# A two-layer encoder trunk on one core: the second overflow test of a block of four experts moves ahead of gather, sums and transposes

## Chip, core and metric

The kernel runs on one core of one Trainium2 chip. The metric is the device time of one execution in microseconds (us), as the median of three runs. The core has five engines: TensorE (PE, its weight loads shown as PEld), VectorE (DVE), ScalarE (ACT), GpSimd (POOL) and SyncE (SP), which here issues the weight transfers. Each has a queue of its own, and an engine works through its queue in order.

## What is computed

Input x is 256 tokens of 1024 float32 values. Two layers follow each other, each with a token mixer and a mixture of 32 experts, and a last normalisation. The change lies in the experts (`hier_moe` of the reference, cut):

```python
g_idx = argmax(xt @ w_rg + b_rg)                 # one of 4 groups per token
top_v, top_i = lax.top_k(e_sel, 2)               # two of the group's 8 experts
gate = ...                                       # 256 x 32, two values per token, the rest 0
for g in range(4):
    h = silu(xt @ w_gate[g]) * (xt @ w_up[g])    # 1024 -> 256, per expert
    h = h * gate[:, g]
    y = y + h @ w_down[g]                        # 256 -> 1024, per expert
x = x + y
```

So each token needs two experts of 32. How many tokens an expert gets is known only once the router has run on the chip.

## The kernel before

**Blocks and slots.** Instead of all 256 tokens, each expert gets a fixed number of token slots. The experts of a layer are worked off in nine blocks, in an order written out by hand (`ORDER`): seven blocks of four experts with 32 slots each, and two blocks of two experts with 64 each. In layer 1 the order is (16, 17), (0 to 3), (18, 19), (4 to 7), (8 to 11), (12 to 15), (20 to 23), (24 to 27), (28 to 31); the text counts these blocks from 0 to 8. The slots of a block fill the 128 rows of TensorE, in four column groups of 32 or two of 64.

**Steps of a block**, in program order:
- `fill_slots` (line 1335 on): transposes of the weighted one-hot table, then ScalarE (line 1341) and VectorE (1342) make the slots' gate values `gs` and the 0/1 matrix `Sm` that maps slots to tokens.
- `gate_up` (line 1442): the gate and up projections into the PSUM tile `gu`, in two halves of the 1024 inputs, one weight page per expert and half. A float32 matmul leaves two records in the trace, so a half has 32.
- `hidden` (1345 on): Silu on ScalarE (1347), then the product with `gs` on VectorE (1348), into the scratch page `scr`.
- Where the next block belongs to a new group: `gather` (1236), which picks that block's tokens with one-hot matrices on TensorE; ScalarE and VectorE evict by turns (`either`, 355 and 359).
- `combine` (1245 on) of the block **before**: its results, kept as a high and a low part, both of the type fp32r, in a `y` page, are summed back to tokens by single-pass matmuls with `Sm` (1251 for the high, 1252 for the low part), and VectorE adds them to x (1253). It comes in two parts, and between them stands `hidden_t`: two transposes of the hidden values (line 372) and their copy by ScalarE (1356).
- `down` (1458): the down projection, in two halves of 512 columns of 32 records each, every half followed by `split_y`: ScalarE writes the high part (1360), VectorE the low part (1361).

**Overflow.** An expert of a block of four may have more than 32 tokens. Slots 33 to 64 are worked off by `second`, under a test of a flag that the router computed (`more`). It stands in two places: the first test (line 1559) between the two halves of `gate_up`, in which the guarded work builds one-hot tables, gathers (1474), fills slots and runs the first half of gate/up for the overflow tokens; the second test (line 1589) ahead of `down`, in which it runs the second half, `hidden`, `hidden_t`, `down` and `combine`. The guarded work has a PSUM tile of its own (`gu2`), but shares `scr` and the `y` page with its block. A test is one unit on all five engines: each branches, and where the flag is 0 PE, DVE and ACT execute one semaphore instruction on the skip path. An expert with more than 64 tokens gets a further stage, the units (tests at line 1424, unit work from 1381 on), once per layer, behind block 3 of layer 0 and block 5 of layer 1.

**Order.** The framework puts the instructions of each engine in an order of its own, close to program order; ready work is put ahead of a test that isn't ready. A test itself is not split, and nothing of its body moves out of it.

**Weights.** All weights stream from HBM through SP into a ring of 25 pages of 1 MB (`pump`, line 227 on). `done` (258) gives a page back behind its last reader and starts the next transfers; a page that a guarded part reads comes free behind the test. `work_page` takes pages of the same ring for `scr`, `y` and the like.

The second test, as it stands before:

```python
y = w["y"] = y_page()
...
if quad:
    with tc.If(more > 0):
        for hf in range(0 if b == 0 else 1, 2):
            second(blk, w, hf)
    done(*[(l, "gu", e, hf) for hf in range(0 if b == 0 else 1, 2) for e in blk])
fn = final(Sm, *y) if end and b == len(blks) - 1 else None
pend = (Sm,) + down(blk, hT, y, next(fn) if fn else None)
```

## Time and profile before

| what | value |
|---|---|
| device time, median of 3 runs | 740.88 us (740.05 to 741.61) |
| profiled execution | 737.13 us |
| its span on the core | 735.4 us |
| PE busy | 631.6 us (86%) |
| DVE busy | 373.7 us (51%) |
| ACT busy | 253.2 us (34%) |
| POOL busy | 107.5 us (15%) |
| moved by DMA | 232.90 MB, mean 317 GB/s |

The profile is of one execution. Its slices cut the span in 40 equal parts of 18.4 us. A line such as L1458 is the program line whose instructions it counts. Behind a duration, `[2.86 <-DVEq L1589]` says that the engine stood idle for 2.86 us before, and that what ended last by the trace was VectorE's queue at line 1589. A name with q (PEq, DVEq, SPq) is an engine's sequencer: branches, semaphores and the issue of transfers.

### The profile page before, as it was taken

The page shows a single profiled execution, that of the slowest core. Times are in us where ns is not written, and L with a number is a line of the kernel's source. Part 1 is how long each engine was busy: PE and PEld are TensorE (multiplying, and loading weights), DVE is VectorE, ACT ScalarE, POOL GpSimd, SP SyncE. Part 2 cuts the span into 40 slices and gives each one's busy share as a digit, 9 for nine tenths or more (in the row PEclk, how much of TensorE's full clock was granted, in tenths as well). Part 3 has the DMA queues.
Part 4 walks back from the last instruction along what each step waited for, and adds up shares of the span by engine and source line. Part 5 has one row for each costly group of instructions (what it writes and reads, how often), then busy time and mean ns, then how long its engine had stood idle before and what let it go on. Part 6 is the DMA issues. An engine that isn't in the chain of part 4 may idle for free. (4 is left out here: it accounts for less than half of the span.)

```text
span 735.4 us, 12004 instructions
## 1 busy us (share of the span) xinstructions
PE 631.6 (86%) x4370; PEld 386.3 (53%) x4370; DVE 373.7 (51%) x899; ACT 253.2 (34%) x578; POOL 107.5 (15%) x135
## 2 busy tenths in 40 slices
PE   7997989889799498598799899989899987769994
PEld 6584877744245334336268677775444434324442
DVE  3899977532334117824279878752423324322424
ACT  3647873421012014524074397352111211001113
POOL 1202001000000021521051754510000000000001
PEclk9999999999899799889999999989999999979998
DMA  8920375896999899999994715895999999998992
GB/s 304 419 108 0 117 289 215 331 389 231 413 406 416 280 405 411 412 415 407 398 417 183 286 59 172 302 362 194 333 416 406 392 410 413 416 366 301 410 382 83
DMA packets 57207, 232.90 MB, mean 317 GB/s; under 512 B 6048, under 2 KB 8480, under 8 KB 48160
## 3 DMA queue, kind: packets, MB, share of 16 engines
q1 hardware_dynamic: 57120, 231.75, 81.5%
q8 instruction: 53, 0.87, 0.5%
q14 instruction: 34, 0.28, 0.1%
HBM read 233.82 MB, written 1.05 MB: 319 GB/s over the span
## 5 line engine op out<-in xcount | busy, mean ns | idle before, releaser
L1442 PE MATMUL gu<-pg,xe 128*32 128x512 f32 (+1 forms) x1024 | 147.9, 618 | 12.4 <-DMA pg<-in_w_up_dram 7.1
L1458 PE MATMUL yp<-pg,scr 128*32 128x512 f32 (+2 forms) x560 | 79.4, 639 | 25.9 <-DVEq L1589 11.5
L1442 PEld LDWEIGHTS gu<-pg,xe 128*32 128x32 f32 (+1 forms) x1024 | 48.1, 117 | 96.7 <-issue 91.0
L1236 PE MATMUL gp<-oh,xn 128*128 128x128 f32 (+1 forms) x416 | 71.2, 325 | 4.0 <-DVE oh L1221 2.0
L1236 PEld LDWEIGHTS gp<-oh,xn 128*128 128x128 f32 x416 | 61.4, 197 | 18.6 <-issue 10.6
L1458 PEld LDWEIGHTS yp<-pg,scr 128*32 128x32 f32 (+1 forms) x560 | 22.1, 120 | 73.0 <-issue 58.2
L1361 DVE TENSOR_TENSOR y<-yp,y 128x512 fp32r<-128x512 f32 (+1 forms) x39 | 26.3, 677 | 65.8 <-ACT y L1360 65.8
L1348 DVE SCALAR_TENSOR_TENSOR scr<-gu,gs,scr 128x256 f32<-128x256 f32 x19 | 9.1, 481 | 97.1 <-ACT scr L1347 97.1
L1228 POOL TENSOR_TENSOR pgt<-oh,gate 128x256 f32<-128x256 f32 (+1 forms) x13 | 10.2, 783 | 316.5 <-PE slp L372 304.6
L1253 DVE TENSOR_TENSOR x<-cp,x 128x512 f32<-128x512 f32 x76 | 48.9, 685 | 14.2 <-PE cp L1252 14.2
L1360 ACT CAST y<-yp 128x512 fp32r<-128x512 f32 (+1 forms) x39 | 22.3, 575 | 88.1 <-PE yp L1458 86.6
L359 DVE TENSOR_SCALAR xe<-gp,vec 128x128 f32<-128x128 f32 (+1 forms) x52 | 20.8, 400 | 52.0 <-PE gp L1236 52.0
L355 ACT ACTIVATE xe<-gp,vec 128x128 f32<-128x128 f32 (+1 forms) x52 | 21.3, 409 | 73.3 <-PE gp L1236 73.2
L1347 ACT ACTIVATE scr<-gu 128x256 f32<-128x256 f32 x19 | 7.3, 384 | 102.3 <-PEq L1559 52.3
L1251 PE MATMUL cp<-y,sm 128*128 128x512 f32 x76 | 34.0, 455 | 0.3 <-PEq L1559 0.2
L1252 PE MATMUL cp<-y,sm 128*128 128x512 f32 x76 | 30.4, 409 | 1.5 <-DVE y L1361 1.5
L1058 DVE SCALAR_TENSOR_TENSOR x<-op,rg,x 128x512 f32<-128x512 f32 x24 | 17.9, 749 | 16.8 <-PE op L681 11.9
L1341 ACT ACTIVATE scr<-slp 128x256 f32<-128x256 f32 x20 | 7.8, 388 | 42.2 <-SPq L1424 28.8
L1251 PEld LDWEIGHTS cp<-y,sm 128*128 128x128 f32 x76 | 14.5, 192 | 10.4 <-issue 8.2
L372 PE MATMUL hp<-cst,scr 128*128 128x128 f32 x40 | 9.3, 314 | 12.2 <-DVE scr L1348 11.1
L372 PE MATMUL slp<-cst,pgt 128*128 128x128 f32 x36 | 8.3, 314 | 11.2 <-DVEq L1424 5.9
L1252 PEld LDWEIGHTS cp<-y,sm 128*128 128x128 f32 x76 | 14.3, 193 | 5.5 <-DVE y L1361 3.8
(454 smaller groups left out, 1209.2 us busy)
## 6 DMA issues: line engine op xcount, KB each, us to landing
pg<-in_w_gate_dram SPq DMA_DIRECT2D x128, 512.0 KB, 10.1
pg<-in_w_up_dram SPq DMA_DIRECT2D x128, 512.0 KB, 10.4
pg<-in_w_down_dram SPq DMA_DIRECT2D x56, 1024.0 KB, 11.8
pg<-in_w_o_dram SPq DMA_DIRECT2D x8, 1024.0 KB, 18.0
pg<-in_w_down_dram SPq DMA_DIRECT2D x12, 512.0 KB, 10.4
pg<-in_w_qk_dram SPq DMA_DIRECT2D x4, 1024.0 KB, 14.9
pg<-in_w_nat_dram SPq DMA_DIRECT2D x4, 960.0 KB, 12.8
wgu<-in_w_gate_dram SPq DMA_DIRECT2D x4, 512.0 KB
```

Of the source, the lines that this page charges most:

```text
L355: S.copy(dst, src) if scale is None else S.activation(dst, src, AF.Copy, scale=scale)
L359: e.tensor_scalar(dst, src, scale, None, op0=OP.mult)
L372: PE.transpose(dst, src, ident[:src.shape[0], :src.shape[0]])
L1058: V.scalar_tensor_tensor(xh, p, rg[:, g, tt:tt + 1], xh, op0=OP.mult, op1=OP.add)
L1236: PE.matmul(p[:, :w], xn[:, tt, k, :], P[:, tt].rearrange("p e c -> p (e c)"), start=(tt == 0), stop=(tt == 1))
L1251: PE.matmul(p, Sm[:, 128 * tt:128 * tt + 128], yh[:, c], start=True, stop=False)
L1252: PE.matmul(p, Sm[:, 128 * tt:128 * tt + 128], yl[:, c], start=False, stop=True)
L1253: V.tensor_tensor(x[:, tt, c], p, x[:, tt, c], OP.add)
L1360: S.copy(yh[:, c], yp)
L1361: V.tensor_tensor(yl[:, c], yp, yh[:, c].bitcast(F32), OP.subtract)
L1442: PE.matmul(gu[m * s:m * s + m, :].rearrange("p (a f) -> p a f", a=2), xs(k, s), page(l, "gu", e, hf)[:, :, k % 4, :], start=(k == 0), sto ...
L1458: PE.matmul(yp[m * s:m * s + m, :], hT[:, j, m * s:m * s + m], page(l, "dn", e)[:, j, c], start=(j == 0), stop=(j == 1), tile_position=(0, ...
```

## The change

The second test and the release of its pages move from ahead of `down` to right behind `hidden`, ahead of the gathers, the sums of the block before, and the block's own transposes. Because the block's hidden values now have to outlive the guarded part, the guarded `hidden` writes to a region of its own in `scr` (from column 1792). The guarded part no longer uses `down`, `split_y`, `combine` and the `y` page: for each half of 512 columns it runs the down matmuls, one eviction by ScalarE or VectorE into `scr`, two sums with `Sm` read as float32, and VectorE's adds to x. The `y` page is taken behind the test.

```diff
-            def hidden(gu, gs):
-                sl, hh = scr[0][:, 1280:1536], scr[0][:, 1536:1792]
+            def hidden(gu, gs, o=1536):
+                sl, hh = scr[0][:, 1280:1536], scr[0][:, o:o + 256]
                 S.activation(sl, gu[:, 0:256], AF.Silu)
                 V.scalar_tensor_tensor(hh, gu[:, 256:512], gs, sl, op0=OP.mult, op1=OP.mult)
                 return hh
...
                 if hf == 1:
-                    hT = hidden_t(hidden(w["gu"], w["S"][1]), 1024)
-                    combine((w["S"][0],) + down(blk, hT, w["y"]))
+
+                    hT = hidden_t(hidden(w["gu"], w["S"][1], 1792), 1024)
+                    y, Sm = scr[0][:, :D], w["S"][0].bitcast(F32)
+                    for c in (slice(0, 512), slice(512, 1024)):
+                        yp = ps("yp2")
+                        for j in range(2):
+                            for s, e in enumerate(blk):
+                                PE.matmul(yp[32 * s:32 * s + 32, :], hT[:, j, 32 * s:32 * s + 32], page(l, "dn", e)[:, j, c],
+                                          start=(j == 0), stop=(j == 1), tile_position=(0, 32 * s))
+                        either(y[:, c], yp)
+                        for tt in range(2):
+                            p = ps("cp")
+                            PE.matmul(p, Sm[:, 128 * tt:128 * tt + 128], y[:, c], start=True, stop=True)
+                            V.tensor_tensor(x[:, tt, c], p, x[:, tt, c], OP.add)
...
                     hh = hidden(gu, gs)
+                    if quad:
+                        with tc.If(more > 0):
+                            for hf in range(0 if b == 0 else 1, 2):
+                                second(blk, w, hf)
+                        done(*[(l, "gu", e, hf) for hf in range(0 if b == 0 else 1, 2) for e in blk])
+
                     for part in range(2):
...
-                    y = w["y"] = y_page()
+                    y = y_page()
...
-                    if quad:
-                        with tc.If(more > 0):
-                            for hf in range(0 if b == 0 else 1, 2):
-                                second(blk, w, hf)
-                        done(*[(l, "gu", e, hf) for hf in range(0 if b == 0 else 1, 2) for e in blk])
```

## Rows read from the trace of the kernel before

**Rows 1.** The page's slices: GB/s in 40 equal parts of the span.
```profile
GB/s 304 419 108 0 117 289 215 331 389 231 413 406 416 280 405 411 412 415 407 398 417 183 286 59 172 302 362 194 333 416 406 392 410 413 416 366 301 410 382 83
```

**Rows 2.** Windows: stretch, length, PE, PEld, DVE, ACT, POOL busy, PEclk, DMA share, GB/s.
```profile
258.00:368.00 110.00, 89.03 (x815) 43.52 (x808) 50.50 (x117) 36.70 (x71) 21.82 (x22) 0.95 1.03 409
524.00:652.00 128.00, 106.47 (x613) 52.53 (x612) 45.95 (x100) 20.40 (x50) 2.72 (x3) 0.98 1.02 409
664.00:716.00 52.00, 48.34 (x380) 23.09 (x380) 15.14 (x28) 8.38 (x22) 0.62 (x1) 1.00 1.01 380
```

**Rows 3.** Waits of SP's queue: who <- releaser: sum us, count, longest.
```profile
SPq L1424 <- SPq L1424: 14.6, 9, 5.2
SPq L247 <- PEq L1589: 9.3, 4, 4.1
```

**Rows 4.** Waits of all engines: the down projection behind line 1589.
```profile
PE yp L1458 <- DVEq L1589: 11.5, 8, 2.9
PE yp L1458 <- ACTq L1589: 5.9, 3, 4.2
```

**Rows 5.** Timeline of PE: start us, us, instruction, records, [idle before <- releaser].
```profile
368.37 1.90 PE L1458 MATMUL yp<-pg,scr 128*32 128x512 f32 x10 [0.22 <-DMA pg<-in_w_down_dram]
...
532.17 5.34 PE L1458 MATMUL yp<-pg,scr 128*32 128x512 f32 x32 [2.86 <-DVEq L1589]
...
618.05 3.62 PE L1458 MATMUL yp<-pg,scr 128*32 128x512 f32 x26 [1.46 <-DMA pg<-in_w_down_dram]
```

**Rows 6.** Timeline of ACT: the slots of block 6, layer 1.
```profile
662.97 0.39 ACT L1341 ACTIVATE scr<-slp 128x256 f32<-128x256 f32 x1 [17.24 <-SPq L1424]
```

**Rows 7.** Instructions of line 1589: ns least/median/most, from, to; idle before.
```profile
L1589 PEldq COMPARE_BRANCH  x15: 78/318/1681, 182.8 to 717.5; - x15
...
L1589 DVEq EVENT_SEMAPHORE  x13: 21/21/21, 189.1 to 719.7; - x13
```

**Rows 8.** Timeline of PE: block 6 of layer 1, whose guarded part runs.
```profile
671.51 0.51 PE L372 MATMUL hp<-cst,scr 128*128 128x128 f32 x2
671.95 3.64 PE L1442 MATMUL gu<-pg,scr 128*32 128x512 f32 x32
676.69 0.51 PE L372 MATMUL hp<-cst,scr 128*128 128x128 f32 x2 [1.10 <-DVE scr L1348]
677.66 3.64 PE L1458 MATMUL yp<-pg,scr 128*32 128x512 f32 x32 [0.46 <-ACT scr L1356]
...
683.34 0.74 PE L1252 MATMUL cp<-y,sm 128*128 128x512 f32 x2 [0.45 <-DVE y L1361]
684.01 3.64 PE L1458 MATMUL yp<-pg,scr 128*32 128x512 f32 x32
```

**Rows 9.** Timeline of ACT: block 6, first eviction of the guarded down projection.
```profile
679.65 0.59 ACT L1360 CAST y<-yp 128x512 fp32r<-128x512 f32 x1 [2.04 <-PE yp L1458]
```

**Rows 10.** Timeline of PE: the unit stage of layer 1, its gather in float32.
```profile
627.31 3.67 PE L1398 MATMUL gpu<-xn,Pu 128*128 128x512 f32 x8 [2.86 <-DVE Pu L1391]
```

**Rows 11.** Timeline of PE: block 7 of layer 1, from gathers to down.
```profile
695.20 2.02 PE L1236 MATMUL gp<-oh,xn 128*128 128x128 f32 x16 [0.18 <-PEq L1559]
...
700.71 0.40 PE L1252 MATMUL cp<-y,sm 128*128 128x512 f32 x1
702.28 1.06 PE L1458 MATMUL yp<-pg,scr 128*32 128x512 f32 x8 [1.17 <-DMA pg<-in_w_gate_dram]
```

**Rows 12.** Timeline of DVE: block 7, the product.
```profile
695.60 0.48 DVE L1348 SCALAR_TENSOR_TENSOR scr<-gu,gs,scr 128x256 f32<-128x256 f32 x1 [5.88 <-ACT scr L1347]
```

**Rows 13.** Timeline of PE: block 8 of layer 1, first sum, transposes, down.
```profile
716.27 0.50 PE L1251 MATMUL cp<-y,sm 128*128 128x512 f32 x1
...
717.35 0.50 PE L372 MATMUL hp<-cst,scr 128*128 128x128 f32 x2
...
719.99 1.50 PE L1458 MATMUL yp<-pg,scr 128*32 128x512 f32 x12 [1.20 <-DVEq L1589]
```

**Rows 14.** Timeline of DVE: block 8, the adds of the sums.
```profile
717.21 2.48 DVE L1253 TENSOR_TENSOR x<-cp,x 128x512 f32<-128x512 f32 x4
```

## The prediction

> **What bounds the kernel now.** I read the page's slices first, then the busy time by stretches, then the waits of the DMA queue (SP) and of TensorE, and last the timelines of the blocks in which a wait could set the end.
>
> The GB/s slices say where the expert stages are: slices 9 to 20 and 29 to 38 run at about 400 GB/s, with dips between [rows 1]. The stretches make it sharper: from 258 to 368 us and from 524 to 652 us the 16 DMA engines are busy to a share of 1.03 and 1.02, at 409 GB/s, while PE has idle time in both (89.0 of 110 us and 106.5 of 128 us busy) [rows 2]. There the weights set the pace. Two rows show that this is not only an average: the last down projection of layer 0 resumes at 368.37 on the landing of a w_down page, and that of block 5 of layer 1 at 618.05 likewise, after a PE wait of 1.46 us [rows 5]. Whatever PE gains ahead of such a row, it waits away there.
>
> Then the picture turns. Behind the unit stage of layer 1, SP stands at the units' skip path (line 1424, 14.6 us in nine waits over both layers) until the transfers in flight have landed [rows 3]; ScalarE starts the slots of block 6 at 662.97 after 17.24 us on that SP branch [rows 6]. From there to the end, blocks 6, 7 and 8 of layer 1 run one behind the other. PE is busy 48.3 of 52 us between 664 and 716 us [rows 2], and its only long gaps are those told below. So the change is paid for, or pays, mainly in these three blocks.
>
> Last, which side of the second test (line 1589) is taken. Its skip path, one semaphore instruction an engine, stands 13 times in the trace, for 14 blocks of four [rows 7]; the fourteenth is block 6 of layer 1, where the guarded part runs [rows 8].
>
> **The change part by part.**
>
> *The waits behind the test.* Before, the first down projection behind line 1589 waits until VectorE has passed the test, which VectorE reaches only behind the adds of the sums of the block before. That is 11.5 us of PE waits in 8 blocks, and 5.9 in 3 more behind ScalarE [rows 4]. After, VectorE passes right behind the product, and the down projection needs only the transposed hidden values. Most of this lies in stretches that the weights bound: block 1 of layer 1 loses 2.86 us ahead of 532.17 [rows 5], but 86 us later block 5 waits for its weights, so I count nothing for it. What counts is block 7 (its last sum ends at 700.71 + 0.40 = 701.11, its down starts at 702.28: 1.17 us [rows 11]) and block 8 (1.20 us ahead of 719.99 [rows 13]).
>
> What is next late there? The transposes. From transposes to down takes 677.66 - 676.69 = 0.97 us where nothing else intervenes [rows 8]; in block 8 the transposes start at 717.35 [rows 13], so their copy frees the down at about 718.3, ahead of the last sum. PE's own sums are then last.
>
> *The moved test itself.* PE drains at a test: at the first test of block 7 the gathers start 0.18 us after the last gate/up matmul [rows 11]. Before, the second drain fell into the wait; after, it falls between gather and sums: +0.2 us a block. The branch itself took 78 to 1681 ns, median 318 [rows 7]; I take it as hidden, because PE's sequencer reaches it while earlier matmuls run; uncovered it costs those 0.3 us, at worst 1.7. So block 7: -1.17 + 0.2 + 0.1 for issue = -0.9 us; block 8: -1.20 + 0.2 = -1.0 us. [...]
>
> *The guarded part, in block 6.* Here the change costs, in three pieces.
> First, the block's own transposes (671.51, 0.44 us until the guarded gate/up goes on) no longer lie inside [rows 8]: the guarded down starts 0.44 us earlier.
> Second, the sums. Before, from the guarded down at 677.66 to the block's own down at 684.01: 6.35 us, both halves of the down first (3.64 us) and then eight single-pass matmuls of 512 columns [rows 8]. After, each half is down, one eviction, two float32 matmuls. Two matmuls of that form, 128x128 by 128x512 in float32, show in the unit stage: four (each leaves two records) take 3.67 us, 0.92 each [rows 10]. Half of the down is 1.82 us; the eviction of the first half started 1.99 us behind the down's start and took 0.59 [rows 9], so a sum can start 2.6 us in; two sums end at 4.4. The second half's first matmuls fit into that wait, the rest (about 1.7) ends at 6.1; its eviction, 0.8 past the down as for the first half, at 6.9; two sums at 8.75. That is +2.4 us.
> Third, the block's own transposes now follow the guarded part, with their copy: +0.97 us before the own down [rows 8].
> Sum: -0.44 + 2.4 + 0.97 = +2.9 us. Below it: if both halves of the down run first, 3.64 + 4 x 0.92 = 7.3 us, +0.95 in place of 2.4, the block costs +1.5; if the own transposes also stay ahead of the test, +0.95. Above: with no overlap at all, and 0.3 to 1.0 us for the branch, +4. I take +2.9, since in program order the first half's sums now stand ahead of the second half's down. The dropped subtraction on VectorE is worth nothing more: it was behind PE's work except for one wait of 0.45 us [rows 8], which the sum holds already.
>
> *Pages released earlier.* The pages of the second gate/up half come free when PE has passed the second test, now some 2 to 6 us earlier. SP waited for that 9.3 us in four issues, at most 4.1 us [rows 3]. But SP keeps several transfers in flight, and the DMA share of 524 to 652 us stays at 1.02 although some of those waits lie in it [rows 2]. Bounds: nothing to -1.5 us; I take -0.2. The DMAs themselves are the same and in the same order; the y page is needed later, not earlier. GpSimd and SP only pass the test (branches, no work).
>
> **The sum:** +2.9 - 0.9 - 1.0 - 0.2 = +0.8 us. Against the profiled execution (737.13 us, span 735.4) that is 737.9; the median of the timed runs stands 3.75 us higher, so 740.88 + 0.8 = **741.7 us**.
>
> **The rivals.**
> *The body orders itself well* (both halves of the down first, or the own transposes ahead): block 6 costs 1.0 to 1.5 in place of 2.9, giving 740.88 - 0.6 = 740.3. For it: that order stands in the trace today; against: today's program order asks for it.
> *The wait moves to the front* (slower): gathers and sums behind the test take PSUM banks that the guarded part used, so PE's first matmul behind the test waits until VectorE has passed it, that is until the product ends. It decides as soon as that first matmul needs such a bank. Block 7's gathers then start not at 695.20 but behind 695.60 + 0.48 [rows 12] plus 0.2 to 0.5, some 1.1 to 1.4 us later; block 8's sums not at 716.27 but behind the product, after which the adds start at 717.21 today [rows 14]: as much. That eats both gains: +2.9 + 0.4 = +3.3, 744.2 us. For it: eight banks and seven tiles in the guarded part; against: at the first test, which is built alike, the gap is 0.18 us [rows 11].
> *Earlier pages do speed the weights* (faster): if a third of SP's 9.3 us [rows 3] is lost transfer time, -3.1 more than counted; 738.4 us.
> [...]
> *It does not do what it says:* the scheduler keeps the skipped test behind the sums, as it already keeps the first test behind gate/up in block 7 [rows 11]; then only the float32 sums show, about 741.8.
>
> **How the numbers follow.** Forecast 0.46 (its own range 740.2 to 743.2); good order in the body 0.18; wait at the front 0.14; earlier pages 0.18; all waits 0.02; no move 0.02. Reaching into the rivals on both sides until 2 in 10 are left out gives 738.7 to 744.2. A measurement of this kernel tells 0.2%, 1.5 us, from no change: faster than 739.4 are most of the earlier-pages case, the all-waits case and a little of the good order, 0.21; slower than 742.4 are the wait at the front and a quarter of the forecast, 0.26; the rest, 0.53, is the same. Cases of both signs stay possible, but none far off.
>
> **What would show it.** Right: the down of blocks 7 and 8 follows the last sum within 0.3 us; block 6 takes about 9 us from guarded down to its own transposes; the down of block 1 of layer 1 starts about 3 us earlier and block 5 still waits for w_down; ScalarE still starts block 6's slots near 663. Wrong: a slots start of block 6 or an end of layer 0 moved by over 1 us (then transfers moved), or gathers that wait for VectorE at the new place of the test.

## The result and the profile after

The changed kernel takes 744.39 us (median of 18 runs), the kernel before 739.58 us in the same series. The medians are 4.8 us apart; over all 18 runs of each the ratio is 1.0075, interval 1.0055 to 1.0095, some 5.5 us slower (4.1 to 7.0). The prediction said 741.7 us, 738.7 to 744.2, most likely no change. The time lies just over the upper end, and the change is clear of noise on the side that had a chance of 0.26. The profiled execution took 743.89 us (span 742.1) against 737.13 us (735.4), so the two traces differ by 6.7 us, more than the medians: the profiled execution of the kernel before is a quick one, 2.45 us under its median, that of the changed kernel lies 0.5 us under its own.

From PE's waits in the changed kernel (who <- releaser: sum us, count, longest; line 1581 is the moved test):

```profile
PE gp L1236 <- DVEq L1581: 7.4, 6, 1.3
PE cp L1251 <- DVEq L1581: 4.7, 4, 1.3
PE gp L1236 <- PEq L1581: 3.3, 1, 3.3
```

The waits of the down projection behind the test (11.5 and 5.9 us, [rows 4]) are gone. 12.1 us put down to VectorE's queue at the test (11.5 before) stand ahead of the first gather or sum instead, 1.2 to 1.3 us in each block: most of the wait has only changed its place.

PE's timeline in block 6 of layer 1 (start us, us, instruction, records, [idle before <- releaser]; line 1500 is the guarded down, 1505 the float32 sums, 1458 the block's own down):

```profile
670.84 0.38 PE L372 MATMUL slp<-cst,scr 128*128 128x128 f32 x2
671.16 7.07 PE L1442 MATMUL gu<-pg,scr 128*32 128x512 f32 x64
...
680.27 1.92 PE L1500 MATMUL yp<-pg,scr 128*32 128x512 f32 x16 [0.46 <-ACT scr L1356]
683.01 1.98 PE L1505 MATMUL cp<-scr,sm 128*128 128x512 f32 x4 [0.81 <-DVE scr L357]
684.92 1.92 PE L1500 MATMUL yp<-pg,scr 128*32 128x512 f32 x16
687.55 1.98 PE L1505 MATMUL cp<-scr,sm 128*128 128x512 f32 x4 [0.70 <-ACT scr L355]
689.37 0.39 PE L372 MATMUL hp<-cst,scr 128*128 128x128 f32 x2
690.22 3.64 PE L1458 MATMUL yp<-pg,scr 128*32 128x512 f32 x32 [0.46 <-ACT scr L1356]
```

The guarded gate/up is no longer cut by the block's own transposes (64 records in one run; [rows 8] had them in two). From the guarded down to the own transposes it takes 689.37 - 680.27 = 9.10 us, where [rows 8] had 6.35 us to the own down.

Block 7 of layer 1, PE's timeline (answers to [rows 11]; the gate/up ends at 701.24):

```profile
702.50 1.80 PE L1236 MATMUL gp<-oh,xn 128*128 128x128 f32 x14 [1.26 <-DVEq L1581]
705.08 0.49 PE L1236 MATMUL gp<-oh,xn 128*128 128x128 f32 x2 [0.78 <-issue]
...
709.05 0.40 PE L1252 MATMUL cp<-y,sm 128*128 128x512 f32 x1
709.38 3.64 PE L1458 MATMUL yp<-pg,scr 128*32 128x512 f32 x32
```

Down follows the last sum at once, as forecast. But PE stood 1.26 us at the test until VectorE had passed it, and then 0.78 us in the midst of the gathers for "issue": nothing that the profile shows. From the end of gate/up to down the block takes 8.14 us; before, 702.28 - 695.02 = 7.26 us (its start from [rows 11], the gate/up's end from the same timeline).

Block 8 (answer to [rows 13]; its gate/up ends at 723.44):

```profile
724.60 0.47 PE L1251 MATMUL cp<-y,sm 128*128 128x512 f32 x1 [1.15 <-DVEq L1581]
...
726.85 2.79 PE L1458 MATMUL yp<-pg,scr 128*32 128x512 f32 x32
```

The sum of the prediction holds no term for layer 0. There the first gather of block 7, and the table matmuls (line 548, work for layer 1's tables) at the start of block 8, read:

```profile
334.69 2.02 PE L1236 MATMUL gp<-oh,xn 128*128 128x128 f32 x16 [3.32 <-PEq L1581]
...
346.31 2.82 PE L548 MATMUL t4p<-ca,tabs 128*32 128x128 f32 x81
352.33 5.01 PE L548 MATMUL t4p<-ca,tabs 128*32 128x96 f32 x128 [3.19 <-issue]
359.08 1.19 PE L548 MATMUL t4p<-ca,tabs 128*32 128x64 f32 x39 [1.75 <-issue]
...
360.44 7.03 PE L1442 MATMUL gu<-pg,xe 128*32 128x512 f32 x59
...
370.87 3.64 PE L1458 MATMUL yp<-pg,scr 128*32 128x512 f32 x32
```

Before, all 256 table records stood ahead of block 8's slots, and its gate/up waited for weights, as in this line of the kernel before:

```profile
357.74 1.91 PE L1442 MATMUL gu<-pg,xe 128*32 128x512 f32 x12 [1.59 <-DMA pg<-in_w_up_dram]
```

Now 252 of the 256 stand behind block 8's slots and its first gate/up matmul. The rest of gate/up, 62 of 64 records, runs only behind nearly all of them, and the last down of layer 0 no longer waits for a w_down page as in [rows 5]: PE sets the end of layer 0, 4.2 us later than before.

Where the 6.7 us of the two traces arise: 3.2 us ahead of block 6 (its slots start at 666.18 instead of 662.97, [rows 6]), 3.0 us in block 6, 0.6 us in blocks 7 and 8.

### The profile page after: what moved, and what is told of

It reads as the page before. It is cut to its first block, busy times and chain, and to the rows that moved or that the text cites. A ratio compares the mean times of both kernels' runs of the same rounds, so it can differ in the third digit from the quotient of the medians.

```text
span 742.1 us, 12038 instructions
## 1 busy us (share of the span) xinstructions
PE 634.2 (85%) x4370; PEld 386.9 (52%) x4370; DVE 373.8 (50%) x898; ACT 250.5 (34%) x576; POOL 106.4 (14%) x135
## 5 line engine op out<-in xcount | busy, mean ns | idle before, releaser
L1442 PE MATMUL gu<-pg,xe 128*32 128x512 f32 (+1 forms) x1024 | 157.0, 624 | 22.0 <-DMA pg<-in_w_up_dram 18.5
L1442 PEld LDWEIGHTS gu<-pg,xe 128*32 128x32 f32 (+1 forms) x1024 | 50.3, 117 | 111.6 <-issue 104.8
L1458 PE MATMUL yp<-pg,scr 128*32 128x512 f32 (+2 forms) x528 | 65.8, 583 | 0.9 <-ACT scr L1356 0.9
L1253 DVE TENSOR_TENSOR x<-cp,x 128x512 f32<-128x512 f32 x72 | 45.8, 684 | 12.8 <-PE cp L1252 12.8
L1251 PE MATMUL cp<-y,sm 128*128 128x512 f32 x72 | 32.1, 450 | 7.1 <-DVEq L1581 4.7
L1458 PEld LDWEIGHTS yp<-pg,scr 128*32 128x32 f32 (+1 forms) x528 | 17.8, 113 | 38.8 <-issue 33.9
L1252 PE MATMUL cp<-y,sm 128*128 128x512 f32 x72 | 28.7, 403 | 0.7 <-DVE y L1361 0.4
L1251 PEld LDWEIGHTS cp<-y,sm 128*128 128x128 f32 x72 | 13.6, 189 | 16.2 <-ACTq L1581 11.5
L548 PE MATMUL t4p<-ca,tabs 128*32 128x32 f32 (+3 forms) x512 | 17.0, 251 | 5.3 <-issue 5.2
L548 PEld LDWEIGHTS t4p<-ca,tabs 128*32 128x32 f32 x512 | 15.4, 117 | 8.1 <-issue 8.0
L1342 DVE TENSOR_SCALAR sm<-slp 128x256 fp32r<-128x256 f32 x20 | 8.4, 422 | 20.1 <-ACT scr L1341 14.8
```

The lines of the kernel that those rows point to most:

```text
L548: PE.matmul(t4p[b][32 * jq:32 * jq + 32, c + lo:c + hi], g0[ri][:, 8 * d + i, :], ca[ri][:, 8 * d + i, m, :].rearrange("p m c -> p (m c)") ...
L1251: PE.matmul(p, Sm[:, 128 * tt:128 * tt + 128], yh[:, c], start=True, stop=False)
L1252: PE.matmul(p, Sm[:, 128 * tt:128 * tt + 128], yl[:, c], start=False, stop=True)
L1253: V.tensor_tensor(x[:, tt, c], p, x[:, tt, c], OP.add)
L1442: PE.matmul(gu[m * s:m * s + m, :].rearrange("p (a f) -> p a f", a=2), xs(k, s), page(l, "gu", e, hf)[:, :, k % 4, :], start=(k == 0), sto ...
L1458: PE.matmul(yp[m * s:m * s + m, :], hT[:, j, m * s:m * s + m], page(l, "dn", e)[:, j, c], start=(j == 0), stop=(j == 1), tile_position=(0, ...
```

## The experiments

The table gives for each kernel the ratio of its time to the kernel before, and five lengths from its trace: from the first gate/up matmul of layer 0 to block 6's slots in layer 1 ("ahead"), and from the same start to the guarded gather of block 6 (line 1474, "to gather"); from there to the end of its own down; from there to the end of block 7's down; from there to the end of block 8's last down.

| kernel | ratio (interval) | ahead | to gather | block 6 | block 7 | block 8 |
|---|---|---|---|---|---|---|
| before | 1 | 513.4 | 514.4 | 23.69 | 18.27 | 19.19 |
| changed | 1.0075 (1.0055 to 1.0095) | 516.4 | 517.4 | 26.70 | 19.16 | 18.92 |
| e1 late test, float32 sums | 1.0056 (1.0024 to 1.0088) | 515.7 | 518.1 | 26.51 | 18.26 | 19.15 |
| e2 early table step | 1.0033 (1.0000 to 1.0065) | 517.8 | 518.8 | 26.69 | 18.70 | 18.95 |
| e3 sums ahead | 1.0078 (1.0042 to 1.0114) | 518.2 | 519.2 | 28.20 | 21.21 | 18.12 |
| e4 one bank | 1.0101 (1.0068 to 1.0134) | 518.5 | 519.5 | 31.16 | 21.21 | 17.99 |
| e5 before, few banks | 0.9979 (0.9947 to 1.0011) | 512.5 | 515.0 | 24.29 | 17.42 | 18.99 |
| e6 changed, few banks | 1.0067 (1.0039 to 1.0095) | 515.1 | 516.1 | 26.69 | 19.89 | 18.47 |
| e7 e6, downs first | 1.0082 (1.0049 to 1.0115) | 517.0 | 518.0 | 24.96 | 19.96 | 18.46 |
| e8 no second test | (one execution) | 513.5 | 515.9 | 10.46 | 17.06 | 26.41 |
| e9 hold | 1.0048 (1.0026 to 1.0071) | 517.1 | 518.1 | 26.69 | 18.90 | 18.94 |
| e10 tables pinned | (one execution) | 520.1 | 521.1 | 26.69 | 18.85 | 18.94 |
| e11 hold and pinned | 1.0045 (1.0021 to 1.0068) | 514.5 | 515.5 | 26.69 | 18.81 | 18.94 |
| e12 e5 with hold | 0.9977 (0.9948 to 1.0007) | 511.1 | 513.6 | 24.28 | 17.42 | 18.99 |
| e13 changed, 64 more | 1.0344 (1.0304 to 1.0383) | 517.1 | 518.1 | 29.45 | 19.18 | 18.94 |
| e14 changed, 32 more | (one execution) | 514.9 | 516.8 | 26.69 | 18.11 | 18.93 |
| e15 e6, 64 more | (one execution) | 516.0 | 517.0 | 28.32 | 19.79 | 18.46 |
| e16 e6, 96 more | (one execution) | 515.8 | 517.9 | 26.69 | 17.66 | 18.45 |

The intervals are about 2.4 us wide to each side, so most verdicts rest on the lengths, which repeat to 0.05 us from block 6 on where the order and the clock are the same. In most traces the gather follows the slots by 0.98 to 0.99 us; in e1, e5, e8, e12, e14 and e16 PE is still at gate/up then, and 1.96 to 2.49 us pass. What counts for the end is the gather.

**Which part of the change costs what.** e1 takes the new guarded part alone, at the old place:

```diff
                 if hf == 1:
-                    hT = hidden_t(hidden(w["gu"], w["S"][1]), 1024)
-                    combine((w["S"][0],) + down(blk, hT, w["y"]))
+                    hT = hidden_t(hidden(w["gu"], w["S"][1]), 1024)
+                    y, Sm = scr[0][:, :D], w["S"][0].bitcast(F32)
+                    for c in (slice(0, 512), slice(512, 1024)):
...
+                        either(y[:, c], yp)
+                        for tt in range(2):
+                            p = ps("cp")
+                            PE.matmul(p, Sm[:, 128 * tt:128 * tt + 128], y[:, c], start=True, stop=True)
+                            V.tensor_tensor(x[:, tt, c], p, x[:, tt, c], OP.add)
```

> The second test at its old place, with the new guarded part (sums in float32, one eviction for each half). Theory (three terms: float32 sums in block 6 of layer 1, a wait of PE at the new place of the test, table work pushed later at the end of layer 0): only the first term is left. In block 6 the stretch from the guarded down projection to the block's own down grows from 6.35 us to about 9.1 us, the waits ahead of down at line 1589 stay, and the time is 2.5 us over the kernel before. Rival (the float32 sums cost nothing, the move costs all): the time is within 1 us of the kernel before.

Measured: 1.0056, some 4 us, 1.8 to 6.5. Its block 6:

```profile
681.12 1.92 PE L1500 MATMUL yp<-pg,scr 128*32 128x512 f32 x16 [0.46 <-ACT scr L1356]
...
690.31 3.64 PE L1458 MATMUL yp<-pg,scr 128*32 128x512 f32 x32
```

9.19 us from the guarded to the own down, 6.35 before: the sums cost 2.84 us, about half of the whole change's price of 5.5 us. The rival is out. But e1 also loses 2.3 us up to the slots and 3.7 us up to the gather, where its program does what the kernel before does; the part on what comes ahead of block 6 returns to it. And by the times e1 (1.0056) and the changed kernel (1.0075) can't be told apart: how much of the slow-down is the move's own is not shown by them.

e2 puts the table step back ahead of the test:

```diff
                     hh = hidden(gu, gs)
+                    if b > TAB_AT and tab is not None:
+                        next(tab, None)
                     if quad:
                         with tc.If(more > 0):
```

> The changed kernel, with the step of the next layer's tables (the copies that feed the table matmuls) back ahead of the second test, where it stood before. Theory: in layer 0 the tables' matmuls no longer push the gate/up projections of block 8, the last down projection of layer 0 ends some 2 us earlier than in the changed kernel (near 372 us instead of 374.5), and the time is 2 to 3 us over the kernel before instead of 5. Rival (weights, through pages and the test of the units, set the end of layer 0): nothing changes, 5 us over the kernel before.

A miss: layer 0's last down ended 225.9 us after the first gate/up matmul (224.8 in the changed kernel, 220.7 before). In PE's queue the tables stood still ahead of all but one of block 8's gate/up matmuls: the edit did not bring back the old order. Its ratio doesn't tell the two theories apart.

**The wait at the test.** e3 gives PE work for the time of Silu and product (`sums_of` runs the four matmuls of the sums' first part and keeps their banks, `add` the adds) and also lets the guarded sums use two banks twice; e4 takes the banks away:

```diff
+                    held = sums_of(pend, 0) if pend is not None else []
                     if quad:
                         with tc.If(more > 0):
...
+                    add(held)
```

> The changed kernel, with the four matmuls of the first part of the sums ahead of the moved test and their adds behind it, so that PE has 1.2 us of work while Silu and product run (the guarded part uses its two sum banks twice). Theory of the wait at the front: PE's idle time at the test falls from 1.25 us to under 0.4 us in the blocks that have sums; blocks 7 and 8 of layer 1 get about 1 us shorter each, and the time is 2 to 3 us under that of the changed kernel, 2.5 us over the kernel before. Rival (draining and branch, not the product, make the idle time): it stays at 1.2 us, the time at 5 us over the kernel before.

```diff
-                        yp = ps("yp2")
+                        yp = w["gu"]
...
-                            p = ps("cp")
+                            p = w["gu"]
```

> The changed kernel, whose guarded second part takes no PSUM bank of its own: transposes, down and sums all go through the bank of the guarded gate/up, one behind the other. Theory (PE waits at the test because the first matmul behind it takes a bank that the guarded part used): the idle time of 1.25 us in the skipped tests falls to 0.2 to 0.5 us; block 6 grows by about 3 us, as nothing overlaps there; the time is about 1 us over that of the changed kernel. Rival (whatever follows a test waits until VectorE has passed it): the idle time stays at 1.25 us and the time is 3 us over that of the changed kernel.

In both the wait for VectorE went: in e4's block 7 the gathers start at 707.31, 0.18 us behind gate/up, though the product is not yet done:

```profile
707.71 0.48 DVE L1348 SCALAR_TENSOR_TENSOR scr<-gu,gs,scr 128x256 f32<-128x256 f32 x1 [5.92 <-ACTq L1584]
```

So in these blocks the matmul behind the test waited not for the test (0.18 us here), but for a bank that the guarded part uses (1.26 us in the changed kernel). The kernel's PSUM pool has eight banks that go round, and the changed guarded part takes seven. The time fell in neither, since another wait came in its place (e3 and e4, block 7):

```profile
707.12 0.27 PE L1236 MATMUL gp<-oh,xn 128*128 128x128 f32 x1
709.40 2.22 PE L1236 MATMUL gp<-oh,xn 128*128 128x128 f32 x15 [2.01 <-issue]
```

```profile
707.31 0.68 PE L1236 MATMUL gp<-oh,xn 128*128 128x128 f32 x4 [0.18 <-PEq L1574]
...
711.63 0.50 PE L1251 MATMUL cp<-y,sm 128*128 128x512 f32 x1 [1.91 <-issue]
```

About 2.0 us without a releaser, where the changed kernel shows 1.26 + 0.78 = 2.04 us for both waits together. The bank's wait had covered most of the other one. Block 7 still took 21.21 us in both, 2.05 us more than in the changed kernel. Most of that is a lower granted clock, 0.79 of full speed from 708 to 716 us in both where the changed kernel had 1.00 from 704 to 712: the second 16 gather records took 3.04 and 3.33 us instead of 1.95. Block 6 has the same (0.79 from 668 to 676 us, the changed kernel 1.00 from 666 to 672): its guarded gathers took 5.34 and 5.28 us instead of 3.84, and without these 1.4 us e4's block 6 grew by the 3 us that were expected. So block 7's length in e3 and e4 says little on the edits; the waits do.

e5 and e6 make the same edit at either place, the guarded sums in two banks (`two`, taken once) twice instead of in four:

```diff
-                            p = ps("cp")
+                            p = two[tt]
```

> The kernel before (test at its old place, its old guarded part), with one edit: the guarded sums take two PSUM banks twice instead of four banks, so that the down projection behind the test no longer gets a bank that the test or the last adds must free. Theory (the wait of 1.2 us ahead of down is a wait for a bank): the waits of down at line 1589, 11.5 us in eight blocks before, fall to under 4 us in all, blocks 7 and 8 of layer 1 get 0.8 us shorter each, block 6 grows by at most 0.7 us, and the time is 1 to 1.5 us under the kernel before. Rival (whatever follows a test waits until VectorE has passed it): the waits stay, and the time is that of the kernel before.

The waits of the old place fell from 17.4 us [rows 4] to 4.2 us, block 7 from 18.27 to 17.42 us, block 8 by 0.2 only, and block 6 grew by 0.60 us:

```profile
701.86 0.40 PE L1252 MATMUL cp<-y,sm 128*128 128x512 f32 x1
702.57 3.64 PE L1458 MATMUL yp<-pg,scr 128*32 128x512 f32 x32 [0.32 <-DVE x L1253]
```

Here 0.32 us is left of the 1.17 us of [rows 11]: in block 7 the late wait too was mostly a wait for a bank, not for the place of the test. In block 8, 0.99 of the 1.20 us stay, and no run shows what holds the down there. The ratio 0.9979 leans to faster and is not told from 1.

> The changed kernel, with the same edit: the guarded float32 sums take two PSUM banks twice. Nothing else moves. Theory of the bank: PE's idle time at the moved test falls from 1.25 us to 0.2 to 0.5 us, except where PE waits for instructions behind the skip (0.8 to 2 us in block 7 of layer 1, which the wait for the product covered in part); block 7 stays within 0.5 us of the changed kernel, block 8 gets up to 1 us shorter, block 6 is the same; the time is 1 us under the changed kernel, 4 us over the kernel before. Rival (a wait for VectorE behind every test): 1.25 us stays.

```profile
698.66 1.12 PE L1236 MATMUL gp<-oh,xn 128*128 128x128 f32 x6 [0.60 <-PEq L1582]
701.87 1.27 PE L1236 MATMUL gp<-oh,xn 128*128 128x128 f32 x10 [2.08 <-issue]
```

At the moved place the same edit frees the bank (0.60 us instead of 1.26), and the wait without a releaser takes 2.08 us: block 7 gets longer, 19.89 us, 0.7 more than the changed kernel where at most 0.5 was expected. Block 8, where no such wait stands, got 0.45 us shorter.

e7 changes the order in the guarded part:

```diff
-                    for c in (slice(0, 512), slice(512, 1024)):
+                    cs = (slice(0, 512), slice(512, 1024))
+                    for c in cs:
                         yp = ps("yp2")
...
                         either(y[:, c], yp)
+                    for c in cs:
                         for tt in range(2):
```

> As the run before (moved test, two banks twice), with both halves of the guarded down projection ahead of the four float32 sums. Theory (in program order each half's sums hold up the second half's down): from the guarded down to the block's own transposes it takes 7.5 us instead of 9.1, and the time is 1.5 us under the run before, 2.5 us over the kernel before. Rival (float32 sums are as slow in any order): 9 us, no gain.

```profile
681.98 3.64 PE L1500 MATMUL yp<-pg,scr 128*32 128x512 f32 x32 [0.46 <-ACT scr L1356]
685.55 3.96 PE L1507 MATMUL cp<-scr,sm 128*128 128x512 f32 x8
689.34 0.39 PE L372 MATMUL hp<-cst,scr 128*128 128x128 f32 x2
```

7.36 us instead of 9.10, as expected: 1.7 us of the price of the sums was the order of four loops. The times of e6 and e7 don't resolve it.

e8 leaves the second test out and with it the guarded projections and sums, so its results are not complete and only its waits count:

> The changed kernel without the second test and without the guarded gate/up, hidden, down and sums (the guarded gathers and slots under the first test stay): results for overflow tokens are left out. One look at what the test itself costs in block 7 of layer 1, from the end of gate/up to the start of down: 7.26 us before, 8.14 us in the changed kernel. Theory (wait for the bank and waiting for instructions both belong to the test): 6.1 to 6.5 us, and no idle time of PE over 0.4 us in between. Rival (gathers and sums alone set it): 7 us or more.

```profile
682.85 2.02 PE L1236 MATMUL gp<-oh,xn 128*128 128x128 f32 x16 [0.21 <-PEq L1570]
...
688.68 1.90 PE L1458 MATMUL yp<-pg,scr 128*32 128x512 f32 x13
```

688.68 - 682.64 = 6.04 us from gate/up to down, and no idle time over 0.21 us. Before, this stretch took 7.26 us, in the changed kernel 8.14. So a test whose work is skipped cost 1.2 us in this block at the old place and 2.1 us at the new one.

**Ahead of block 6.** SP's timeline at the units' test of layer 0, in the kernel before and then in the changed one (issues of weight transfers; SP stands at the skip between the last two):

```profile
243.45 0.33 SPq L247 DMA_DIRECT2D pg<-in_w_gate_dram  x1
248.90 0.33 SPq L247 DMA_DIRECT2D pg<-in_w_up_dram  x1
```

```profile
244.73 0.33 SPq L247 DMA_DIRECT2D pg<-in_w_gate_dram  x1
245.10 0.43 SPq L247 DMA_DIRECT2D pg<-in_w_up_dram  x1
252.34 0.33 SPq L247 DMA_DIRECT2D pg<-in_w_gate_dram  x1
```

In the kernel before, the DMA share is 0.06 from 248.0 to 248.5 us and 0.00 from there to 249.0: SP issues again when the transfers in flight have landed. The up half of one page moved ahead of the test, and 5.45 us without an issue became 7.23 us. The same stands in e1 (8.14 us, test at the old place) and in e8 (7.33 us, no second test). e9 holds that page back (the pages of block 3's w_down are given back there, but start nothing yet), e10 keeps the tables in program order, e11 does both, e12 holds in e5:

```diff
-                    done(*[(l, "dn", e) for e in blk])
+                    if l == 0 and b == UNIT_AT[l]:
+                        for e in blk:
+                            del st["tiles"][(l, "dn", e)]
+                            st["ns"] -= 1
+                    else:
+                        done(*[(l, "dn", e) for e in blk])
```

```diff
-                            PE.matmul(t4p[b][32 * jq:32 * jq + 32, c + lo:c + hi], g0[ri][:, 8 * d + i, :],
+                            pin(PE.matmul(t4p[b][32 * jq:32 * jq + 32, c + lo:c + hi], g0[ri][:, 8 * d + i, :],
```

> The changed kernel; in layer 0 the pages of block 3's w_down start no new transfer until the units' test is passed. In the kernel before, the last gate/up page ahead of that test had its gate half ahead of the test and its up half behind it; in the changed kernel both stand ahead, and SP waits at the skip until they have landed (7.2 us from the last issue to the next, 5.5 before). Theory (this one transfer more delays the weights of layer 0 by 1.5 to 2 us): from the last issue to the next it takes 5.5 us again, the second gate/up half of block 5 has landed 114 to 115 us after the first gate/up matmul of block 0 (114.0 before, 115.6 in the changed kernel), block 6's slots in layer 1 come 1 to 1.5 us earlier against that matmul, and the time is 1.5 us under the changed kernel, 4 over the kernel before. Rival (the moved test and the tables alone delay layer 0): no change.

> The changed kernel with the table matmuls of line 548 kept in program order, so that in layer 0 they all run between block 7's down and block 8's slots, as in the kernel before. Theory (tables between and ahead of block 8's gate/up cost 2 us at the end of layer 0): the last down of layer 0 ends 222 to 223 us after the first gate/up matmul of block 0 (224.8 in the changed kernel, 220.7 before). Rival (weights and the test set it): 224 to 225 us.

> Both edits together. Theory: all that the changed kernel lost ahead of block 6 of layer 1 comes back; block 6's slots start 513 to 514.5 us after the first gate/up matmul of layer 0 (513.4 before, 516.4 in the changed kernel), and the time is 3.5 us over the kernel before: the guarded part (3 us) and blocks 7 and 8 (0.6 us) are left. Rival (something else ahead of block 6): 516 us, and 5 us over the kernel before.

> The kernel before with the guarded sums in two banks twice and with the transfers of block 3's w_down pages held behind the units' test. Theory (one transfer less in flight at the test frees SP sooner, but the transfer itself then comes later): the stretch from last issue to next is 5 to 5.7 us as before, the landings of layer 0 stay within 0.5 us, and the time is that of the same kernel without the hold, 1.5 us under the kernel before. Rival (every transfer held back there is lost): the landings come 1 us later, and the time is that of the kernel before.

The stretch without an issue became 4.78 us in e9, 4.36 in e11, 4.12 in e12. The weights gained less: block 5's second half had landed 115.5, 114.8 and 112.9 us after the first gate/up matmul (115.7 changed, 114.0 before and in e5). e9 alone gained nothing ahead of block 6, e10 was worse than the changed kernel (its last down of layer 0 ended at 227.0, not 222 to 223), e11 came to 514.5 as expected, and e12, of which no gain was expected, gained 1.4 us on e5 ahead of block 6, without a time that can be told from e5's. The two edits at the new place fit the theory together but not one by one. And e11's profiled execution is the quickest of its 12 (739.94 us, median 743.06), e9's is not (743.83, median 743.40), so the 514.5 is weak support, and the hold is not shown to help at either place.

A reason not to read more into single profiles there: the same gathers of block 0 of layer 0, in the changed kernel and in e2, whose programs are alike up to there:

```profile
166.41 3.62 PE L1236 MATMUL gp<-oh,xn 128*128 128x256 f32 x16
```

```profile
166.62 5.30 PE L1236 MATMUL gp<-oh,xn 128*128 128x256 f32 x16
```

The granted clock from 166 to 172 us was 1.00 in the first and 0.72 in the second, behind the same idle time of 1.83 us. Such a drop costs 1.7 us in one execution and nothing in the other. The pair of main traces has one of its own, in the gather of the units' stage of layer 1, which takes 3.67 us in [rows 10] and more in the changed kernel:

```profile
629.60 5.40 PE L1398 MATMUL gpu<-xn,Pu 128*128 128x512 f32 x8 [3.04 <-DVE Pu L1391]
```

The granted clock was 1.00 in the kernel before and 0.68 in the changed one. All other traces but e13's (3.70 us) show 5.09 to 6.73 us here, e5 and e12 at the old place as well (5.26 and 5.09). Block 6's first gate/up went the other way: 9.71 us at a granted clock of 0.73 in the kernel before, 8.15 us at 0.86 in the changed one.

**The wait without a releaser.** Four runs shift all later instructions of PE by 32, 64 or 96 tiny matmuls at the start and change nothing else. These did not fit into PE's first wait, as I had thought: 64 of them took 25 us, most of it at a granted clock of 0.50, so the times (1.0344 for e13) say nothing, and only the places of the waits count.

```diff
     for i in range(14):
         PE.matmul(warm[:, :128], ones, ones, start=True, stop=True)
+    for i in range(64):
+        PE.matmul(warm[:, :8], ones, ones[:, :8], start=True, stop=True)
```

> The changed kernel with 64 matmuls of 8 columns more at the start, while PE waits for its first weights (a write to an unused bank). Theory (PE waits for instructions: a packet of 16384 B of the instruction queue starts behind the taken branch, and PE goes on 2.5 us behind that start): the waits behind the moved test move to other blocks; the 3.3 us in block 7 of layer 0 falls to the 1.25 us of the bank, or the 0.8 us in block 7 of layer 1 goes, and others appear elsewhere; wherever one stands, a packet of 16384 B starts 2.4 to 2.6 us ahead of its end. The time moves by up to 2 us either way. Rival (the waits belong to the test or to the skipped length): all stand where they stood.

> As the run before with 32 matmuls: a second place of the pieces. Theory: a third pattern of waits, each with its packet 2.4 to 2.6 us ahead of its end. Rival: the pattern of the changed kernel.

> The changed kernel with the guarded sums in two banks twice, and 64 tiny matmuls at the start. Theory: the wait of 2.08 us in the middle of block 7's gathers moves or goes, and without it block 7 of layer 1 takes 17.8 us from down to down (19.9 with it, 19.2 in the changed kernel, 18.3 before). Rival: 2.1 us stay and block 7 takes 19.9 us.

> The same with 96 tiny matmuls: another place of the pieces. Theory: if the wait stood in block 7 with 64, it is gone here or stands elsewhere; 17.8 us for block 7 where no packet starts behind its branch. Rival: 2.1 us stay in block 7.

The trace lists the packets of the instruction queue q8 (16384 B each, 53 in the changed kernel). Against the ends of some of PE's idle times they stand so (us):

```
kernel    place                 idle   until    packet starts   before the end
changed   layer 0, block 7      3.32   334.69   331.91          2.78
changed   layer 0, tables       3.19   352.33   349.79          2.54
changed   layer 1, block 7      0.78   705.08   702.53          2.54
e6        layer 1, block 7      2.08   701.87   699.42          2.45
e13       layer 1, block 7      0.79   729.93   727.34          2.58
e14       layer 0, block 2      4.22   210.75   207.90          2.85
e14       layer 0, block 5      3.30   280.68   277.93          2.75
e15       layer 1, block 7      1.99   727.52   725.09          2.42
```

The changed kernel's other such idle times over 0.6 us fit: 5.85, 2.91 and 1.75 us in layer 0, with a packet 2.88, 2.50 and 2.38 us ahead of their ends. The kernel before has three (5.29, 4.34 and 1.58 us; 2.97, 2.31 and 2.56 us). The match is not without exceptions: some idle times of 0.6 to 0.8 us at the test, in e6, e7, e15 and e16, have no packet there.

With 32 more matmuls the wait in block 7 of layer 1 is gone (18.11 us), and two that the changed kernel doesn't have stand in layer 0. With 96 more, e16's block 7 takes 17.66 us, 2.2 us less than e6's. That is the shortest block 7 of all with the moved test; e5, with the test at its old place, takes 17.42 us. With 64 more, block 7's pattern is that of none (0.79 and 1.99 us again): 64 of these matmuls leave 128 matmuls and 128 weight loads, and the run has one packet more, 54; all six idle times of the changed kernel are back at their places in e13, though not all with their lengths (1.48 instead of 3.32 us in block 7 of layer 0). So with one packet more the pattern came back. That 64 of these matmuls shift the code by just one packet is my estimate from 54 against 53; the number of packets doesn't simply grow with the code (e14 has 55, e16 56), and no run shows how many instructions a packet holds. For e13 and e15 alone my expectation, that the waits move, was wrong, and the rival's words fit; with e14 and e16 beside them the rival falls.

## Why the prediction was wrong

The prediction's sum was +0.8 us, against 5.5 us by the times. What the forecast named as signs that it is wrong all came: block 6's slots 3.2 us later, the end of layer 0 4.2 us later, and gathers that wait for VectorE at the new place.

- **Block 6: right, in part by luck.** Forecast +2.9 us, measured 26.70 - 23.69 = +3.0. By its pieces: the own transposes out of the way -0.60 (forecast -0.44; from the slots' transposes to the guarded down 9.43 us, 10.03 before), the sums +2.75 (forecast +2.4; the second half's down stood behind the first half's sums as a whole, no part of it in the wait; by the prediction's own numbers 2.6 - 1.82 = 0.8 us of that down fit into the wait, which leaves 1.0 us and not its 1.7, so that its rows give about +1.7 us, and the slip made up for an overlap that didn't come), the own transposes behind them 0.85 (forecast 0.97). e1 and e7 show that sums and order are the cause.
- **Blocks 7 and 8: the step that failed.** Forecast -0.9 and -1.0, measured +0.89 and -0.27. The old wait went, as said, and down followed the last sum. But the forecast priced the moved test as a drain of 0.2 us and held the branch hidden, while the first matmul behind it needs a bank of the guarded part and waited 1.15 to 1.26 us. That was the rival "the wait at the front": mechanism, condition and price (1.1 to 1.4 us; measured 1.15 to 1.26) were right, at a chance of 0.14. The evidence set against it, 0.18 us at the first test [rows 11], was the wrong row: the first guarded part takes three of the eight banks, and the gathers behind it got banks that had long been free. It said nothing on a part that takes seven. The 0.1 us for issue that the forecast adds in block 7 is shown by no run: the last sum's record ends at 709.05 + 0.40 = 709.45 in the changed kernel, and down starts at 709.38.
- **The branch: mis-sized.** "Hidden, at worst 1.7 us" came from the old place [rows 7], where PE's sequencer passes the test while PE still has sums or gathers to run: in the kernel before, all 15 branches at line 1589 begin ahead of the end of the matmul that runs then, the longest (1.68 us at 362.85) while PE works until 364.17. At the new place nine of 15 begin only when PE has run empty, block 7's at 701.46 with gate/up done at 701.24, and idle times that by the packets of q8 I put down to waiting for code lie open: 0.78 us in block 7 beside the bank's wait, 2.0 to 2.1 us without it, and most of the 3.32 us in layer 0.
- **Earlier pages: the order of the transfers did change.** Forecast -0.2 us; the stretch ahead of block 6 grew by 3.0 us in the traces. "The same transfers in the same order" did not hold: one transfer came ahead of the units' test, and SP stood longer. That it stood there at all was read in [rows 3]; that the change reaches it was not.
- **Layer 0 was not covered.** [Rows 5] show that the end of layer 0 waited for weights, but by 0.22 us only. The table step lay between the sums and the old test, and the prediction named no queue effect for it.
- **Open.** From the trace, 3.0 us of the slow-down arise ahead of block 6, and no term of the prediction covers them; from the times, 5.5 - 3.6 = about 2 us (0.5 to 3.4). The thirteen traces with the moved test show 515.5 to 521.1 us up to the guarded gather, the three with the old place and the old form of the sums 513.6 to 515.0. But e8, without the second test, shows 515.9, and e1, with the old place, 518.1; in both the transfer came ahead of the units' test as well. e1's trace also has 70.1 us of this stretch at a granted clock of 0.50, the kernel before 52.5, the changed kernel 46.6. So transfer order, the wait for code, tables and the clock all differ there, but no run shows how much of the 3.0 us each has, and none that the moved test is the cause. Nor is it known why the new form of the guarded part alone (e1) moves that transfer.

## What to carry over

Before a conditional part is moved, list what the instruction behind its new place takes from the part: banks above all. If buffers go round, a skipped part still holds its place in the round, and giving it fewer banks shortened block 7's wait at either place (1.17 to 0.32 us, 1.26 to 0.60 us) without moving anything. Move a branch only where the engine has work queued when its sequencer passes it; here a queue that had run empty laid open waits of 0.8 to 2.1 us in block 7 of layer 1. Before two single traces are compared, compare their granted clocks stretch by stretch, and ask how quick each profiled execution was among its kernel's runs. And compare the order of every queue, that of the transfers first, since a scheduler may reorder work that the edit never names.

The best kernel of this study is the one before with the guarded sums in two banks (0.9979) or with the hold as well (0.9977); neither interval excludes 1.

## What the hardware showed that was not expected

- Packets of 16384 B on queue q8 start 2.4 to 2.9 us ahead of the ends of the idle times in the table. That they carry PE's code is read from their number and from the shifts: 53 in the changed kernel, 54 with 64 matmuls more, 42 in e8, whose guarded part is shorter.
- In these runs the place of such waits moved with the length of the code ahead of them: 32 tiny matmuls at the start took the wait out of a block some 700 us later (19.16 to 18.11 us) and put waits of 4.2 and 3.3 us into two others.
- A float32 matmul of 128x128 by 128x8 leaves two records. In e13 these follow each other every 0.112 us at a granted clock of 0.99 and every 0.213 us at 0.50, so one matmul cost 0.22 or 0.43 us; all 128 records took 24.97 us. The clock fell 2.6 us into these matmuls, with PE busy all the time.
